# Strassen weight sums by accumulating DMAs in place of GpSimd additions in a two-layer decoder trunk

## The chip, the cores and the metric

The kernel runs on one core of a Trainium2 chip. The metric is the device time of one execution in microseconds (us); less is better. The engines are named as the profile names them: PE (TensorE, matrix products; PEld are its weight loads), DVE (VectorE), ACT (ScalarE), POOL (GpSimd) and SP (SyncE, which here only issues transfers). Each engine works through its own queue in order. Transfers between device memory and on-chip memory run on 16 shared DMA engines; an engine issues a transfer and goes on, and whoever needs the data waits on a semaphore.

## The reference

A decoder trunk of two layers on 512 tokens of width 1024, all float32. Each layer is a token mixer, a cross-attention into 256 memory tokens, and a squared-ReLU MLP with 4096 hidden channels; each is added to the residual stream after an RMSNorm.

```python
for layer in range(DEPTH):                      # DEPTH = 2
    h = h + mixer(rmsnorm(h, ...), ...)         # RG-LRU + FoX attention, or dilated + sliding-window attention
    h = h + memory_cross_attention(rmsnorm(h, ...), mem, ...)
    h = h + squared_relu_mlp(rmsnorm(h, mlp_norm[layer]), mlp_w_up[layer], mlp_w_down[layer])
return rmsnorm(h, final_norm)

def squared_relu_mlp(h, w_up, w_down):
    return jnp.square(jax.nn.relu(h @ w_up)) @ w_down
```

The change touches `h @ w_up` alone.

## The kernel before

Activations are held transposed: channels on the 128 partitions, the 512 tokens along the free axis. Every float32 product is made of three faster ones: each operand is split into a high and a low part (`hi_lo`: ACT copies it to the rounded type, L156; DVE subtracts, L157), and `mm3` issues high x high (L177), high x low (L178) and low x high (L179).

The MLP of a layer runs in four quarters of the hidden channels (`for qd in range(4)`). A quarter is four units of up-projection and then eight down-projections. A unit (class `Unit`) is a block product by a Strassen-Winograd scheme with seven products, `p1` to `p7`; its weight operands are A11, A12 and A22 (parts 0, 1 and 3 of the stored weight block) as they are loaded, and four sums formed on the chip, S1 to S4, into which part 2 goes as well. Each product is twelve matmuls of 128x128 by 128x256; each down-projection is 24 matmuls of 128x128 by 128x512. Over the kernel there are 2 layers x 4 quarters x 4 units = 32 units.

`Unit.load`, called first in `p1`, brings the weights in. It uses four tiles, each of 128 partitions:

- `d1` (printed as `wr`; 1024 columns): part 0 (A11) in the lower half, S1 in the upper. Two buffers, shared with the weight tiles of all other projections.
- `d2` and `d3` (printed as `d`; 1024 columns): A12 and S2, A22 and S4. They share four buffers (tag `v`), so that two units' pairs fit.
- `e` (printed as `ptl`; 512 columns): S3. Four buffers.

Four loads of 256 KB are issued by SP (L965). Four GpSimd additions follow (L968): S1 = part 2 + part 3, S3 = part 2 + part 0 (on top of part 2 in `e`), S2 = S1 + part 0, S4 = S2 + part 1. `Unit.weight` converts a tile when a product first asks for one of its operands: ACT to `wh`, DVE to `wl` (three buffers each). Both halves of a tile are converted by one instruction each, so a conversion of `d2` waits for A12 and S2. `d2` is asked for by `p2`, `d3` by `p4`.

The Tile scheduler sets the order of instructions on each engine from the written order and priorities; loads of weights have a raised priority (`tc.high_priority(200)`), so they stand on SP's queue as early as their buffers allow. The product steps of neighbouring units are woven into one another. In steady state, `d2` of one unit, `d2` of the next and `d2` of the third use one and the same of the four `v` buffers in turn, so that each load of `d2` waits for the conversion of the `d2` before.

Of the kernel before, what the change touches and what calls it, by code (L numbers as in the profile page):

```python
# [13 lines left out]
ALU = mybir.AluOpType  # L14
# [22 lines left out]
def build(ctx, tc, a):  # L37
    nc = tc.nc
    V, A, G, T, SY = nc.vector, nc.scalar, nc.gpsimd, nc.tensor, nc.sync
# [14 lines left out]
    def t2k(tag, dt=F32, shape=None):  # L54
        cnt[0] += 1
        return wk.tile(shape or [128, 512], dt, tag=tag, name=f"{tag}_{cnt[0]}", bufs=BUFS[tag])
# [893 lines left out]
    class Unit:  # L950
# [5 lines left out]
        def load(self):  # L956
            with tc.high_priority(200):
                cnt[0] += 1
                i = cnt[0]
                d1 = wp.tile([128, 1024], F32, tag="wr", name=f"wr_{i}", bufs=2)  # L960
                d2, d3 = (wk.tile([128, 1024], F32, tag="v", name=f"d{x}_{i}", bufs=BUFS["v"]) for x in (2, 3))
                e = t2k("ptl")
                lo, hi = slice(0, 512), slice(512, 1024)
                for part, dst in ((2, e), (3, d3[:, lo]), (0, d1[:, lo]), (1, d2[:, lo])):
                    SY.dma_start(out=dst, in_=self.src[part])  # L965
                for out, x, y in ((d1[:, hi], e, d3[:, lo]), (e, e, d1[:, lo]), (d2[:, hi], d1[:, hi], d1[:, lo]),
                                  (d3[:, hi], d2[:, hi], d2[:, lo])):
                    G.tensor_tensor(out=out, in0=x, in1=y, op=ALU.add)  # L968
            self.raw = {"d1": (d1, ("A11", "S1")), "d2": (d2, ("A12", "S2")), "d3": (d3, ("A22", "S4")), "e": (e, ("S3",))}

        def weight(self, name):
# [436 lines left out]
```

## Time and profile before

| | |
|---|---|
| device time, median of 3 runs | 1479.89 us (1478.21 to 1481.08) |
| the profiled execution | 1479.2 us, its span 1477.2 us |
| PE busy | 1425.7 us, 97% of the span |
| PE weight loads | 1234.2 us, 84% |
| DVE busy | 1073.5 us, 73% |
| ACT busy | 747.2 us, 51% |
| POOL busy | 361.9 us, 24% |
| transfers | 143.03 MB, mean 97 GB/s |

The two microseconds between the span and the execution's time lie around the span. The profile gives for each engine its busy time; the chain of waits that ended last runs over PE for 75% of the span and over DVE for 16%. The 128 GpSimd additions are among POOL's 361.9 us; POOL also does the sums of squares of the norms (L270), the last step of their roots (L298) and the division of the softmax (L348). A row of the timeline gives the start and the length of an instruction; for a transfer the length is that of its issue, and the landing is given apart.

### The profile page before, as it was taken

How to read it: one execution, taken by the hardware profiler on the slowest of the kernel's cores; microseconds unless marked ns; L12 is line 12 of the kernel's file. 1: busy time of each engine (PE TensorE's matmuls, PEld its weight loads, DVE VectorE, ACT ScalarE, POOL GpSimd, SP SyncE). 2: the span in 40 equal slices, each digit the busy share in tenths (PEclk: the TensorE clock that was granted, in tenths of full speed). 3: DMA queues.
4: the chain of work that ended last, by engine and by line, in shares of the span. 5: the costliest groups of instructions: out<-in, count | busy, mean ns of one | idle time of the engine just before them, and what ended most of it. 6: DMA issues, size and time to landing. Idle time of an engine off the chain costs nothing.

```text
span 1477.2 us, 21427 instructions
## 1 busy us (share of the span) xinstructions
PE 1425.7 (97%) x8064; PEld 1234.2 (84%) x8064; DVE 1073.5 (73%) x1733; ACT 747.2 (51%) x1321; POOL 361.9 (24%) x300
## 2 busy tenths in 40 slices
PE   7999999999899999999999999999998999999996
PEld 5777887888798989889887888788878889898985
DVE  7788876656885867678678989855497667586773
ACT  4777754545452534435457867644354435252452
POOL 3003221002613315051213313200054041422303
PEclk9999999999999999999999999999998999999998
DMA  5222214423132333422332231333222424242221
GB/s 191 83 86 86 73 65 150 136 93 129 50 115 87 117 92 87 134 58 71 110 108 69 79 94 64 100 131 126 100 93 76 125 65 128 72 122 93 72 86 57
DMA packets 55558, 143.03 MB, mean 97 GB/s; under 512 B 6816, under 2 KB 12320, under 8 KB 55456
## 3 DMA queue, kind: packets, MB, share of 16 engines
q1 hardware_dynamic: 54368, 140.63, 30.1%
q8 instruction: 63, 1.03, 0.3%
q10 hardware_dynamic: 1088, 1.05, 0.2%
q14 instruction: 39, 0.32, 0.1%
HBM read 136.15 MB, written 2.10 MB: 94 GB/s over the span
## 4 chain that ended last, share of the span: by engine, by line
PE 75%; DVE 16%; ACT 5%; issue 3%; POOL 0%; DMA 0%; DVEq 0%; ACTq 0%; POOLq 0%
PE mm L177 18%; PE mm L178 18%; PE mm L179 18%; DVE wl L157 4%; PE s L177 3%; PE s L178 2%; PE s L179 2%; PE t L354 2%; PE pv L177 1%; PE pv L178 1%; PE pv L179 1%; ACT wh L156 1%; DVE hT L474 1%; PE mm L233 1%; PE mm L234 1%
## 5 line engine op out<-in xcount | busy, mean ns | idle before, releaser
L156 ACT ACTIVATE wh<-wr 128x1024 fp32r<-128x1024 f32 x214 | 226.1, 1058 | 296.1 <-PE mm L178 224.3
L157 DVE TENSOR_TENSOR wl<-wr,wh 128x1024 fp32r<-128x1024 f32 x214 | 289.0, 1354 | 73.8 <-ACT wh L156 72.1
L177 PE MATMUL mm<-acth,wh 128*128 128x512 f32 (+1 forms) x768 | 299.1, 392 | 0.9 <-DVE hT L474 0.8
L178 PE MATMUL mm<-actl,wh 128*128 128x512 f32 (+1 forms) x768 | 297.9, 388 | 0.1
L179 PE MATMUL mm<-acth,wl 128*128 128x512 f32 (+1 forms) x768 | 297.6, 388 | 0.0
L177 PE MATMUL mm<-hgh,wh 128*128 128x512 f32 (+1 forms) x504 | 188.3, 374 | 7.6 <-ACT hgh L156 6.7
L178 PE MATMUL mm<-hgl,wh 128*128 128x512 f32 (+1 forms) x504 | 185.5, 368 | 4.7 <-DVE hgl L160 3.7
L179 PE MATMUL mm<-hgh,wl 128*128 128x512 f32 (+1 forms) x504 | 184.8, 367 | 0.3
L177 PEld LDWEIGHTS mm<-acth,wh 128*128 128x128 f32 x768 | 144.0, 188 | 30.5 <-ACT acth L156 2.0
L179 PEld LDWEIGHTS mm<-acth,wl 128*128 128x128 f32 x768 | 144.3, 188 | 29.2
L178 PEld LDWEIGHTS mm<-actl,wh 128*128 128x128 f32 x768 | 144.5, 188 | 27.7 <-DVE actl L157 0.7
L270 POOL TENSOR_TENSOR ssq<-ssq,sq 128x512 f32<-128x512 f32 (+1 forms) x48 | 67.2, 1401 | 409.2 <-ACT sq L258 408.8
L348 POOL TENSOR_SCALAR p<-p,den 128x256 f32<-128x256 f32 (+1 forms) x96 | 66.6, 699 | 254.5 <-DVE den L347 190.1
L1053 DVE TENSOR_TENSOR kv<-mm,Rt 128x512 f32<-128x512 f32 x56 | 38.7, 690 | 109.7 <-PE mm L179 109.7
L177 PEld LDWEIGHTS mm<-hgh,wh 128*128 128x128 f32 x504 | 96.5, 191 | 21.9 <-ACT hgh L156 7.1
L968 POOL TENSOR_TENSOR wr<-ptl,d 128x512 f32<-128x512 f32 x32 | 43.9, 1372 | 283.5 <-DVE wl L157 246.3
L178 PEld LDWEIGHTS mm<-hgl,wh 128*128 128x128 f32 x504 | 96.5, 192 | 18.5 <-DVE hgl L160 4.4
L179 PEld LDWEIGHTS mm<-hgh,wl 128*128 128x128 f32 x504 | 96.4, 191 | 14.6 <-DVE wl L157 0.7
L157 DVE TENSOR_TENSOR wl<-d,wh 128x1024 fp32r<-128x1024 f32 x64 | 87.0, 1359 | 22.1 <-ACT wh L156 21.8
L156 ACT ACTIVATE wh<-d 128x1024 fp32r<-128x1024 f32 x64 | 67.4, 1053 | 58.0 <-PE mm L178 42.2
L177 PE MATMUL s<-hgh,wh 128*128 128x256 f32 (+1 forms) x272 | 80.8, 297 | 3.8 <-DVE kv L1008 2.2
L179 PE MATMUL s<-hgh,wl 128*128 128x256 f32 (+1 forms) x272 | 79.7, 293 | 0.0
(322 smaller groups left out, 3297.2 us busy)
## 6 DMA issues: line engine op xcount, KB each, us to landing
wr<-in_mlp_down SPq DMA_DIRECT2D x64, 512.0 KB, 3.3
d<-in_mlp_up SPq DMA_DIRECT2D x64, 256.0 KB, 2.6
wr<-in_cd_w_in SPq DMA_DIRECT2D x18, 512.0 KB, 3.4
wr<-in_xa_q SPq DMA_DIRECT2D x16, 512.0 KB, 3.3
wr<-in_xa_k SPq DMA_DIRECT2D x16, 512.0 KB, 3.3
wr<-in_xa_v SPq DMA_DIRECT2D x16, 512.0 KB, 3.3
wr<-in_xa_w_o SPq DMA_DIRECT2D x16, 512.0 KB, 3.4
ptl<-in_mlp_up SPq DMA_DIRECT2D x32, 256.0 KB, 3.0
```

The costliest lines, as they stand in the source:

```text
L156: A.activation(out=hi, in_=src, func=AF.Copy)
L157: V.tensor_tensor(out=lo, in0=src, in1=hi.bitcast(F32), op=ALU.subtract)
L177: T.matmul(ps, lhsT=wh, rhs=xh, start=start, stop=False, **kw)
L178: T.matmul(ps, lhsT=wh, rhs=xl, start=False, stop=False, **kw)
L179: T.matmul(ps, lhsT=wl, rhs=xh, start=False, stop=stop, **kw)
L233: T.matmul(st["ps"][b], lhsT=xh, rhs=h[:, k2, :], start=k == 0, stop=False)
L234: T.matmul(st["ps"][b], lhsT=xh, rhs=lo[:, k2, :], start=False, stop=False)
L270: eng.tensor_tensor(out=self.ssq, in0=self.ssq, in1=q, op=ALU.add)
L348: G.tensor_scalar(out=p, in0=p, scalar1=dens[:, i:i + 1], scalar2=1.0, op0=ALU.mult, op1=ALU.mult)
L354: T.transpose(ps[:, c:c + 128], src, ident)
L968: G.tensor_tensor(out=out, in0=x, in1=y, op=ALU.add)
L1053: V.tensor_tensor(out=t, in0=ps, in1=Rt, op=ALU.mult)
```

## The change

The four additions go. Part 2 is loaded not only into `e` but also into the upper halves of `d1`, `d2` and `d3`, and transfers that add to what lies at their destination (`accum_op=ALU.add`), issued by GpSimd, bring the other parts on top: one for S1 (part 3), one for S3 (part 0), two for S2 (parts 3 and 0), three for S4 (parts 3, 0 and 1). Per unit there are then seven plain loads and seven accumulating transfers of 256 KB each instead of four loads and four additions; over the kernel 224 and 224 instead of 128 and 128.

```diff
--- before.py
+++ after.py
@@ -961,11 +961,10 @@
                 d2, d3 = (wk.tile([128, 1024], F32, tag="v", name=f"d{x}_{i}", bufs=BUFS["v"]) for x in (2, 3))
                 e = t2k("ptl")
                 lo, hi = slice(0, 512), slice(512, 1024)
-                for part, dst in ((2, e), (3, d3[:, lo]), (0, d1[:, lo]), (1, d2[:, lo])):
+                for part, dst in ((2, e), (3, d3[:, lo]), (0, d1[:, lo]), (1, d2[:, lo]), (2, d1[:, hi]), (2, d2[:, hi]), (2, d3[:, hi])):
                     SY.dma_start(out=dst, in_=self.src[part])
-                for out, x, y in ((d1[:, hi], e, d3[:, lo]), (e, e, d1[:, lo]), (d2[:, hi], d1[:, hi], d1[:, lo]),
-                                  (d3[:, hi], d2[:, hi], d2[:, lo])):
-                    G.tensor_tensor(out=out, in0=x, in1=y, op=ALU.add)
+                for part, dst in ((3, d1[:, hi]), (0, e), (3, d2[:, hi]), (3, d3[:, hi]), (0, d2[:, hi]), (0, d3[:, hi]), (1, d3[:, hi])):
+                    G.dma_start(out=dst, in_=self.src[part], accum_op=ALU.add)
             self.raw = {"d1": (d1, ("A11", "S1")), "d2": (d2, ("A12", "S2")), "d3": (d3, ("A22", "S4")), "e": (e, ("S3",))}
 
         def weight(self, name):
```

Several accumulating transfers to the same half-tile go one after another: each waits until the one before has landed. Lines behind L965 stand one lower in the changed kernel.

On POOL, in the second quarter of the first layer, this is the place of its third and fourth unit (790 and 807 in the names; 855 and 866 are `e` tiles, 854 the `d` tiles of the next quarter). Before:

```order
L968 TENSOR_TENSOR wr_790_4805<-ptl_791_4808,d3_790_4807 128x512
L968 TENSOR_TENSOR ptl_791_4808<-ptl_791_4808,wr_790_4805 128x512
L968 TENSOR_TENSOR d2_790_4806<-wr_790_4805 128x512
L968 TENSOR_TENSOR d3_790_4807<-d2_790_4806 128x512
L968 TENSOR_TENSOR wr_807_4940<-ptl_808_4943,d3_807_4942 128x512
L968 TENSOR_TENSOR ptl_808_4943<-ptl_808_4943,wr_807_4940 128x512
L968 TENSOR_TENSOR d2_807_4941<-wr_807_4940 128x512
L968 TENSOR_TENSOR d3_807_4942<-d2_807_4941 128x512
```

The same place on POOL now ("x2" and "x3" are so many like instructions in a row, each waiting for the one before):

```order
L967 DMA wr_790_4841<-in_mlp_up 128x512
L967 DMA d3_790_4843<-in_mlp_up 128x512 x3
L967 DMA wr_807_4982<-in_mlp_up 128x512
L967 DMA ptl_855_5455<-in_mlp_up 128x512
L967 DMA d2_790_4842<-in_mlp_up 128x512 x2
L967 DMA d3_807_4984<-in_mlp_up 128x512
L967 DMA ptl_866_5539<-in_mlp_up 128x512
L967 DMA d3_807_4984<-in_mlp_up 128x512 x2
L967 DMA d2_807_4983<-in_mlp_up 128x512
L967 DMA d3_854_5454<-in_mlp_up 128x512
L967 DMA d2_807_4983<-in_mlp_up 128x512
```

Where one addition filled a half of `d2`, two transfers in sequence do; those of `d2` stand behind the three of an earlier `d3`, and they no longer need the sum in `wr`.

On SP, the loads of the same place. Before:

```order
L965 DMA wr_790_4805<-in_mlp_up 128x512
L965 DMA d3_790_4807<-in_mlp_up 128x512
L965 DMA wr_807_4940<-in_mlp_up 128x512
L965 DMA ptl_855_5407<-in_mlp_up 128x512
L965 DMA d2_790_4806<-in_mlp_up 128x512
L965 DMA d3_807_4942<-in_mlp_up 128x512
L172 DMA wr_825_5076<-in_mlp_down 128x1024
L965 DMA ptl_866_5485<-in_mlp_up 128x512
L965 DMA d2_807_4941<-in_mlp_up 128x512
L965 DMA d3_854_5406<-in_mlp_up 128x512
```

SP now:

```order
L965 DMA wr_790_4841<-in_mlp_up 128x512 x2
L965 DMA d3_790_4843<-in_mlp_up 128x512 x2
L965 DMA wr_807_4982<-in_mlp_up 128x512 x2
L965 DMA ptl_855_5455<-in_mlp_up 128x512
L965 DMA d2_790_4842<-in_mlp_up 128x512 x2
L965 DMA d3_807_4984<-in_mlp_up 128x512 x2
L172 DMA wr_825_5124<-in_mlp_down 128x1024
L965 DMA ptl_866_5539<-in_mlp_up 128x512
L965 DMA d2_807_4983<-in_mlp_up 128x512 x2
L965 DMA d3_854_5454<-in_mlp_up 128x512 x2
```

The order on SP is the same, with two loads for each of `wr`, `d2` and `d3` where one stood. On PE, ACT and DVE the order of the products and conversions around this place is that of before but for swaps of neighbours.

## Rows read from the trace of the kernel before

**Rows 1.** Busy times by window, the second quarter of the first layer's MLP.

```profile
core 0: us, PE busy (x) PEld busy (x) DVE busy (x) ACT busy (x) POOL busy (x), PEclk, DMA share, GB/s
478.00:562.00 84.00, 83.72 (x528) 75.87 (x527) 59.45 (x68) 33.38 (x48) 25.04 (x16) 1.00 0.34 101
```

**Rows 2.** PE's waits (total, times, longest): 340 to 430 us; 430 to 700; 1110 to 1160.

```profile
PE mm L177 <- ACT hgh L156: 3.4, 1, 3.4
PE pv L177 <- DVE kv L1014: 2.6, 1, 2.6
...
PE s L177 <- DVE kv L1027: 0.4, 2, 0.3
...
PE pv L177 <- DVE kv L1014: 2.2, 1, 2.2
```

**Rows 3.** Timeline (start us, length us) of DVE around 395 us, first quarter; line totals of the additions.

```profile
392.77 0.68 DVE L157 TENSOR_TENSOR kv<-ssq,kv 128x512 fp32r<-128x512 f32 x1
393.60 2.08 DVE L157 TENSOR_TENSOR wl<-d,wh 128x1024 fp32r<-128x1024 f32 x1 [0.16 <-ACT wh L156]
395.61 1.78 DVE L157 TENSOR_TENSOR qkl<-E,qkh 128x512 fp32r<-128x512 f32 x1
...
398.74 1.75 DVE L157 TENSOR_TENSOR wh<-ptl,wh 128x512 fp32r<-128x512 f32 x1
...
L968 POOL TENSOR_TENSOR wr<-ptl,d 128x512 f32<-128x512 f32 x32 | 43.9, 1372 | 283.5 <-DVE wl L157 246.3
```

**Rows 4.** Timeline of SP, loads of `d` in quarters one (415) and two.

```profile
477.51 0.33 SPq L965 DMA_DIRECT2D d<-in_mlp_up  x1
488.39 3.11 SPq L965 DMA_DIRECT2D d<-in_mlp_up  x2
500.63 3.14 SPq L965 DMA_DIRECT2D d<-in_mlp_up  x2
...
415.13 3.12 SPq L965 DMA_DIRECT2D d<-in_mlp_up  x2
```

**Rows 5.** Transfers, issue to landing: L965's min/median/max, then medians by tile, with KB.

```profile
DMA to landing us min/median/max: 2.4/2.6/5.8
...
d<-in_mlp_up SPq DMA_DIRECT2D x64, 256.0 KB, 2.6
wr<-in_mlp_down SPq DMA_DIRECT2D x64, 512.0 KB, 3.3
kv<-in_memT SPq DMA_DIRECT2D x12, 256.0 KB, 4.1
```

**Rows 6.** Timeline of ACT and DVE: conversions of `d` in the second quarter.

```profile
486.00 1.06 ACT L156 ACTIVATE wh<-d 128x1024 fp32r<-128x1024 f32 x1 [2.30 <-PE mm L178]
498.01 1.05 ACT L156 ACTIVATE wh<-d 128x1024 fp32r<-128x1024 f32 x1
...
517.09 1.05 ACT L156 ACTIVATE wh<-d 128x1024 fp32r<-128x1024 f32 x1
...
487.10 1.23 DVE L157 TENSOR_TENSOR wl<-d,wh 128x1024 fp32r<-128x1024 f32 x1 [1.83 <-ACT wh L156]
```

**Rows 7.** Timeline of PE: first low-part matmul of `p2`, quarters two and one.

```profile
501.05 0.28 PE L179 MATMUL pv<-hgh,wl 128*128 128x256 f32 x1
511.13 0.28 PE L179 MATMUL pv<-hgh,wl 128*128 128x256 f32 x1
...
426.61 0.28 PE L179 MATMUL pv<-hgh,wl 128*128 128x256 f32 x1
```

**Rows 8.** Busy times by window around PE's longest wait; columns as in rows 1.

```profile
384.00:386.00 2.00, 0.00 (x0) 0.00 (x0) 2.00 (x4) 1.83 (x4) 0.00 (x0) 1.00 0.00 0
...
388.00:390.00 2.00, 1.53 (x7) 1.53 (x8) 2.00 (x3) 1.21 (x3) 0.00 (x0) 0.50 0.20 77
390.00:392.00 2.00, 2.00 (x11) 2.00 (x11) 1.98 (x4) 0.82 (x3) 1.53 (x1) 0.50 0.40 80
392.00:394.00 2.00, 2.00 (x15) 2.00 (x14) 1.84 (x4) 2.00 (x4) 0.99 (x1) 0.70 0.14 51
```

## The prediction

> **What bounds the kernel now.** The change lives in the eight MLP quarters, so I read one of them first. Over the 84 us of the second quarter PE is busy 83.72 us at full clock; DVE is busy 59.45, ACT 33.38, POOL 25.04, and the DMA engines have a share of 0.34 [rows 1]. So PE bounds a quarter, and relieving DVE or POOL shortens it only where PE waits for them. The list of PE's waits is the second view: from 430 to 700 us, three quarters long, the largest entry is 0.4 us. Only the first quarter of each layer has a wait that the additions could cause: `p2`'s bank `pv` waits for DVE's `kv` for 2.6 us in layer 0 and 2.2 us in layer 1. The 3.4 us for `hgh` is the norm, before any product [rows 2]. The most that the change can gain is therefore about 5 us. What it can lose is set by how far ahead of PE the weights are, and the third view is the timeline of the loads, conversions and matmuls of `d2`.
>
> **What it removes.** 128 GpSimd additions of about 1.37 us, some 176 us of POOL's time. In the first quarter DVE's conversions beside them take 2.08, 1.78 and 1.75 us. Free of them, the 128x512 form took 0.68 and the 128x1024 form takes 1.23 [rows 3, 6]. The excess of those three is 0.85 + 1.10 + 1.07 = 3.0 us, more than the wait of 2.6. I take both waits as gone, 2.6 + 2.2 = 4.8 us. The products behind them are PE's own work, and nothing else is late there. With no effect on those waits the term is 0.
>
> **What it adds on SP.** 96 more plain loads at 0.33 us of issue each [rows 4], spread over 8 x 84 us. SP waits for buffers between loads, so this costs nothing but a shift of 0.33 us for the second load of a half-tile; that shift is in the sums below. If that cover went, it would be 32 us at the very most.
>
> **What it adds on the path: serial accumulating transfers.** Half of `d2` was filled by one addition that could start as soon as its buffer came free. It now needs a load of part 2 and then two accumulating transfers, the second issued after the first has landed. Call the time from issue to landing of one such transfer L. No row shows one. The nearest rows are these: a plain load of 256 KB lands after 2.6 us; one of 512 KB after 3.3; one of 256 KB from `in_memT`, a different shape of the same size, after 4.1 [rows 5]. An accumulating transfer has to read its destination as well and is put in by GpSimd. So the low end is 2.6, and the high end two 512 KB transfers one after another, 6.6. I take 4.1, the slowest 256 KB row: same bytes, more work than the plain one. This choice is the weakest step of the whole sum.
>
> Conversion of `d2` takes 2.3 us, from ACT's start at 486.00 to DVE's end at 488.33 [rows 6], and that frees the buffer for the `d2` of the next unit. In the second quarter:
>
> - Unit 2: loads from 488.39, landed at 488.39 + 0.33 + 2.6 = 491.3, sums complete at 491.3 + 2L [rows 4, 5]. PE wants the low half at 501.05 [rows 7], so the conversion must start by 498.7 (it started at 498.01, [rows 6]). Delay 2L - 7.4, at L = 4.1 it is 0.8 us.
> - Unit 3, same buffer: the conversion ends at 493.6 + 2L, the loads land 2.9 later, and two more transfers follow: 496.6 + 4L. PE wants it at 511.13 [rows 7], conversion by 508.8. Total delay 4L - 12.2 = 4.2 us, of which 3.4 come as a second wait. If unit 2 was in time, its buffer comes free at 500.63 as before [rows 4] and the delay is 2L - 5.2, zero up to L = 2.6.
> - The first quarter has only one such step: loads from 415.13 [rows 4], sums at 418.1 + 2L, wanted at 426.61 - 2.3 = 424.3 [rows 7]. Delay 2L - 6.2 = 2.0 us.
>
> The loads have no slack of their own to hide this. They are issued the moment the buffer comes free, and a unit's twelve-matmul products go on at PE's pace. Six quarters have the two-step chain (quarters two to four of both layers, whose loads I take to repeat the pattern of rows 4): 6 x 4.2 = 25 us, plus 2 x 2.0 = 4 us.
>
> `d3` takes three transfers in a row, but is wanted later: the third unit's comes with the `d2` load at 491.2 and its conversion starts at 517.09 [rows 6]. It is not late for any L up to 6.6. On POOL, however, it is ahead of others. The `d3` of unit 2, loaded at 477.51 [rows 4], issues its third transfer at 480.4 + 2L, and the `d2` transfers of unit 2 stand behind it. At L = 4.1 that is 488.6, before 491.3, so free; at 6.6 it is 493.6, 2.3 us late, 14 us in six quarters. In the first quarter the norm's root (L298) and its sums of squares (L270) stand among the transfers on POOL, and the root is behind the last transfer to the `d2` of unit 2 there. I cost that at nothing, since the loads of that unit are the ones that find their buffers empty; without that cover it is one transfer's time, L, once a layer.
>
> **Clock.** Each PE wait of some length has a second price. After the 3.4 us wait PE ran at a granted clock of 0.50 for 4 us (388 to 392) and 0.70 for 2 us, that is 1.2 GHz and a mixture [rows 8]. It lost 4 x 0.5 + 2 x 0.3 = 2.6 us. The second wait of the chain is as long, 3.4 us, so 6 x 2.6 = 16 us. The bounds are 0, if shorter waits leave the clock alone (the 2.6 and 2.2 us waits are in the trace beside it), and 16.
>
> **The sum at L = 4.1.** 25 + 4 + 16 - 5 = +40 us on the profiled execution's 1479.2, whose own time is 0.7 below the median: 1479.9 + 40 = 1520. At L = 2.6: -5, 1475. At L = 3.5: six delays of 1.8 and two of 0.8, too short for the clock, 12 - 5 = +7, 1487. At L = 6.6: 6 x 14.2 + 2 x 7.0 = 99, + 14 + 16 - 5 = +124, 1604.
>
> The Trainium skill speaks against so large a number. Its page "Collectives: The Full Stack", section "The bandwidth ceiling: the fold count and why AG ≠ RS ≠ AR", says that an add in the transfer engines needs two source reads and so runs at half the rate of a copy. By that and the fixed cost on the page "DMA: Bandwidth & Descriptors", section "Anatomy of one DMA — SWDGE (gpsimd) path" (about 2.0 us plus bytes over 436 GB/s), I estimate L = 2.0 + 2 x 0.6 = 3.2 and a sum of 6 x 1.2 + 2 x 0.2 - 5 = +3 us. No row here shows an accumulating transfer, so I stay with 4.1.
>
> **Rivals.**
> A. *The accumulating transfer lands like a plain one, L = 2.6 to 2.7.* Then nothing of the chain is late, and the relief of DVE is all that is left: 1479.9 - 5 = 1475, faster. For it: same bytes, and 2.6 is the median of all loads of this tile. Against it: the transfer reads its destination too, and its issue is GpSimd's work. It decides at L = 2.7, where the delays begin to eat the 5 us; from 2.7 to 3.0 the result is within 0.2%. The section on the SWDGE path just named, without the second read, gives this very case: 2.0 + 0.6 = 2.6 us, an estimate.
> B. *The DMA engines fill up.* A share of 0.34 over 84 us is 28.6 us of engine time for 32 pieces of 256 KB (16 up, 16 down) [rows 1], 0.9 us each. After the change a quarter has 44 plain pieces and 28 accumulating ones. Counted once: 72 x 0.9 = 64 us, fits in 84. Counted twice: 100 pieces, 89 us, 5 us too much a quarter, 40 in all, close to the forecast's own sum. Counted 2.5 times: 114 pieces, 102 us, 18 us too much, 8 x 18 = 143, about 1620. Three times: 240 us. For it: transfers nearly double in bytes and the destination is read. Against it: the share would have to be nearly three times what it is.
> C. That the change does not do what it says is ruled out: the order on POOL holds 224 accumulating transfers and none of the 128 additions.
>
> **How the numbers follow.** The forecast (a serial chain with L above 3.0 and up to 6.6) gets 0.68, of which L = 4.1 is the likeliest; rival A 0.19 (0.10 faster, 0.09 within 0.2%, which is 3 us and about what a measurement of this kernel can tell from no change); rival B, with engines that are the bound, 0.13. Predicted 1520. The range leaves out A's faster part and half of B and of the longest L, some 0.2: 1477 to 1620. Faster 0.10, same 0.09, slower 0.81.
>
> **What would show it.** The landing time of the transfers at the changed line (4.1 forecast, under 2.8 for A). In the second quarter: PE's waits at `pv` for `wh` or `wl` of `d2`, 0.8 us and then 3.4 us with a clock of 0.5 behind it; in the first quarter one of 2 us; the old waits for `kv` gone; DVE's conversions of 128x1024 all near 1.23 us. For B: a DMA share near 1 and plain loads landing late. The forecast is wrong if L is not what I took, if the third and fourth quarter's chain differs from the second's, or if the transfers get in each other's way long before the engines are full.

## The result, and the profile after

The changed kernel takes 1621.51 us (median of 4 runs, 1614.72 to 1623.53) against 1480.49 us; the ratio is 1.094, with a 95% interval of 1.090 to 1.098. The forecast was 1520 us with a range of 1477 to 1620: slower, as forecast, but by 141 us where 40 were worked out, and just past the end of the range.

The profiled execution has a span of 1621.7 us. The first section of its page (busy us, share of the span, instructions):

```profile
PE 1463.9 (90%) x8064; PEld 1266.3 (78%) x8064; DVE 1002.2 (62%) x1733; ACT 744.5 (46%) x1321; POOL 353.3 (22%) x396
```

PE's 8064 matmuls take 1463.9 us where they took 1425.7. The span is 144.5 us longer: 38 of it are the same matmuls at a lower clock, and 106 are PE standing idle. What it waits for (engine and the bank it writes, line, producer: us in total, times, longest), over the whole span:

```profile
PE pv L177 <- ACT wh L156: 96.2, 14, 10.1
PE mm L177 <- ACT hgh L156: 10.5, 2, 5.3
PE s L177 <- DVE kv L1007: 8.2, 2, 4.5
...
PE pv L179 <- DVE wl L157: 5.4, 14, 0.5
```

Fourteen waits of `pv` for `wh`: in `p2`, for the conversion of `d2`, two in each of six quarters (15.7 us together in the second) and one in each first quarter (5.0 and 6.0), 96.2 us and 5.4 for `wl`. None of them is in [rows 2]. The old waits of `pv` for DVE's `kv` (2.6 and 2.2 us, [rows 2]) are gone; a wait of `s` for `kv` (L1007) of some 4 us in each first quarter has come (the section on why the prediction was wrong follows it up). Of the 106 us of idling, 101.6 are the waits for `d2`.

The second quarter, which the prediction was worked out for, by the same window as [rows 1]. Columns: PE, PEld, DVE, ACT and POOL busy us (instructions), granted clock, DMA share, GB/s:

```profile
478.00:562.00 84.00, 67.60 (x433) 62.68 (x432) 39.14 (x53) 27.40 (x43) 20.99 (x24) 0.88 0.76 175
```

PE does 433 matmuls in the window where it did 528, the clock is 0.88 where it was 1.00, and the DMA share is 0.76 where it was 0.34. The quarter stands some 15 us later now, by the waits before it (the loads of unit 2's `d2` are at 503.26 where they were at 488.39), so this window still holds the end of the first quarter. Moved by 15 us, to 493 to 577, it shows the same clock and 432 matmuls, and a DMA share of 0.83 at 191 GB/s.

The transfers (tile, source, issuing queue, count, KB, median us from issue to landing), and min/median/max of the accumulating ones alone. They answer to [rows 5]:

```profile
d<-in_mlp_up POOLq DMA_DIRECT2D x160, 256.0 KB, 5.7
d<-in_mlp_up SPq DMA_DIRECT2D x128, 256.0 KB, 4.1
...
DMA to landing us min/median/max: 3.8/5.7/11.1
```

L is 5.7 us and not 4.1, and the plain load before it takes 4.1 where it took 2.6.

Now the chain in the second quarter, in the timeline of SP, POOL, ACT and PE (start us, length us; in brackets the idle time before and who ended it). They answer to [rows 4, 6, 7]:

```profile
492.43 0.80 SPq L965 DMA_DIRECT2D d<-in_mlp_up  x2
...
503.26 5.15 SPq L965 DMA_DIRECT2D d<-in_mlp_up  x4
...
498.45 0.86 POOL L967 DMA_DIRECT2D d<-in_mlp_up  x1 [5.60 <-DVE wl L157]
504.22 0.86 POOL L967 DMA_DIRECT2D d<-in_mlp_up  x1 [4.91 <-DMA d<-in_mlp_up]
510.14 0.86 POOL L967 DMA_DIRECT2D d<-in_mlp_up  x1 [5.06 <-DMA d<-in_mlp_up]
510.73 1.17 POOL L967 DMA_DIRECT2D wr<-in_mlp_up  x1
511.26 1.52 POOL L967 DMA_DIRECT2D ptl<-in_mlp_up  x1
511.80 1.88 POOL L967 DMA_DIRECT2D d<-in_mlp_up  x1
520.20 1.75 POOL L967 DMA_DIRECT2D d<-in_mlp_up  x2 [6.52 <-DMA d<-in_mlp_up]
...
524.39 1.06 ACT L156 ACTIVATE wh<-d 128x1024 fp32r<-128x1024 f32 x1 [12.94 <-DMA d<-in_mlp_up]
...
525.50 0.58 PE L177 MATMUL pv<-hgh,wh 128*128 128x256 f32 x1 [10.10 <-ACT wh L156]
```

The plain loads of unit 2's `d2` are issued at 503.26 (the row's other two loads are unit 3's `d3`). The order in the section on the change says whose the POOL rows are: 498.45, 504.22 and 510.14 are the three transfers to `d3` of unit 2, the second and third issued when the one before has landed; 511.80 is the first to `d2`, 520.20 the second. The conversion starts at 524.39, 21.1 us after the loads. In the kernel before it had to start 498.7 - 488.39 = 10.3 us after them to be in time [rows 4, 7]. So it is 10.8 us late, and PE waits 10.1. The prediction said 0.8 for this step. The 21.1 us are three pieces:

- 8.5 us from the loads to the first transfer's issue, where 2.9 were counted. GpSimd's queue stood at `d3` until 510.14.
- 8.4 us from the first to the second transfer, where L = 4.1 was counted. It was issued within 1.7 us of the three before it, as soon as the queue moved.
- 4.2 us for the second transfer, as counted.

The clock behind this wait, by windows (columns as above); it answers to [rows 8]:

```profile
524.00:526.00 2.00, 0.50 (x2) 0.51 (x2) 0.52 (x1) 1.61 (x3) 0.00 (x0) 0.50 1.04 171
526.00:528.00 2.00, 1.54 (x8) 1.25 (x7) 2.00 (x3) 2.00 (x3) 0.86 (x1) 0.50 0.57 88
528.00:530.00 2.00, 2.00 (x11) 2.00 (x11) 2.00 (x4) 0.40 (x2) 0.00 (x0) 0.50 0.94 192
530.00:532.00 2.00, 2.00 (x11) 2.00 (x11) 0.24 (x1) 0.36 (x1) 0.38 (x1) 0.50 1.05 333
532.00:534.00 2.00, 2.00 (x17) 2.00 (x16) 0.69 (x1) 0.91 (x3) 1.62 (x3) 0.88 1.07 396
```

PE runs at half its clock (1.2 GHz) until about 532, as it did after the 3.4 us wait of before.

### The profile page after: what moved, and what is told of

The parts are those of the page before. It is cut to its first block, busy times and chain, and to the rows that moved or that the text cites. A ratio compares the mean times of both kernels' runs of the same rounds, so it can differ in the third digit from the quotient of the medians.

```text
span 1621.7 us, 21819 instructions
## 1 busy us (share of the span) xinstructions
PE 1463.9 (90%) x8064; PEld 1266.3 (78%) x8064; DVE 1002.2 (62%) x1733; ACT 744.5 (46%) x1321; POOL 353.3 (22%) x396
## 3 DMA queue, kind: packets, MB, share of 16 engines
q0 software_dynamic: 32256, 58.73, 22.9%
## 4 chain that ended last, share of the span: by engine, by line
PE 60%; DVE 11%; DMA 10%; issue 10%; ACT 5%; POOL 3%; SPq 0%; POOLq 0%; DVEq 0%; ACTq 0%
PE mm L177 15%; PE mm L178 15%; PE mm L179 15%; DMA d<-in_mlp_up 8%; DVE wl L157 3%; ACT wh L156 2%; DMA wr<-in_mlp_up 2%; POOL d L967 2%; PE s L177 2%; PE s L178 2%; PE s L179 1%; PE t L354 1%; PE pv L179 1%; PE pv L177 1%; PE pv L178 1%
## 5 line engine op out<-in xcount | busy, mean ns | idle before, releaser
L157 DVE TENSOR_TENSOR wl<-wr,wh 128x1024 fp32r<-128x1024 f32 x214 | 264.1, 1236 | 88.0 <-ACT wh L156 85.7
L967 POOL DMA_DIRECT2D d<-in_mlp_up x160 | 144.1, 964 | 625.9 <-DMA d<-in_mlp_up 486.6
L177 PE MATMUL mm<-hgh,wh 128*128 128x512 f32 (+1 forms) x504 | 189.0, 375 | 11.3 <-ACT hgh L156 10.5
L157 DVE TENSOR_TENSOR wl<-d,wh 128x1024 fp32r<-128x1024 f32 x64 | 77.8, 1221 | 150.6 <-ACT wh L156 150.6
L178 PEld LDWEIGHTS mm<-actl,wh 128*128 128x128 f32 x768 | 144.5, 188 | 27.8 <-DVE actl L157 0.7
L177 PE MATMUL pv<-hgh,wh 128*128 128x256 f32 x128 | 46.2, 361 | 96.6 <-ACT wh L156 96.2
L177 PEld LDWEIGHTS pv<-hgh,wh 128*128 128x128 f32 x128 | 31.8, 248 | 99.6 <-ACT wh L156 99.1
L270 POOL TENSOR_TENSOR ssq<-ssq,sq 128x512 f32<-128x512 f32 (+1 forms) x48 | 71.5, 1490 | 161.1 <-ACT sq L258 160.4
```

The lines of the kernel that those rows point to most:

```text
L157: V.tensor_tensor(out=lo, in0=src, in1=hi.bitcast(F32), op=ALU.subtract)
L177: T.matmul(ps, lhsT=wh, rhs=xh, start=start, stop=False, **kw)
L178: T.matmul(ps, lhsT=wh, rhs=xl, start=False, stop=False, **kw)
L270: eng.tensor_tensor(out=self.ssq, in0=self.ssq, in1=q, op=ALU.add)
L967: G.dma_start(out=dst, in_=self.src[part], accum_op=ALU.add)
```

## Experiments

Two theories stood after the result. The first is the forecast's: serial transfers on the way from a free buffer of `d2` to its conversion. The second is the rival that the DMA engines are full. It had gained weight: its price of 1620 us is what was measured. That price counted an accumulating transfer as 2.5 plain ones; what it takes is on the page, queue by queue (packets, MB, share of 16 engines over the span):

```profile
q1 hardware_dynamic: 68192, 165.80, 31.3%
q0 software_dynamic: 32256, 58.73, 22.9%
```

22.9% of 1621.7 us for 224 accumulating transfers is 1.66 us of all engines each, twice the 0.83 us of an average plain 256 KB in the kernel before (30.1% of 1477.2 us for 140.63 MB). Counted twice, the prediction's own sum for this rival was 40 us, and the loss is 141; but the engines' share was high enough to ask.

All times are medians; ratios are to runs of the kernel before beside them, with 95% intervals.

### S2 by GpSimd, the rest by transfers (e1), and S4 by GpSimd, the rest by transfers (e2)

Edits against the changed kernel, its lists of transfers written out one by one, e1:

```diff
-SY.dma_start(out=d2[:, hi], in_=self.src[2])
-for part, dst in ((3, d2[:, hi]), (0, d2[:, hi])):
-    G.dma_start(out=dst, in_=self.src[part], accum_op=ALU.add)
+G.tensor_tensor(out=d2[:, hi], in0=d1[:, hi], in1=d1[:, lo], op=ALU.add)
```

and e2:

```diff
-SY.dma_start(out=d3[:, hi], in_=self.src[2])
-for part, dst in ((3, d3[:, hi]), (0, d3[:, hi]), (1, d3[:, hi])):
-    G.dma_start(out=dst, in_=self.src[part], accum_op=ALU.add)
+G.tensor_tensor(out=d3[:, hi], in0=d2[:, hi], in1=d2[:, lo], op=ALU.add)
```

> S2 goes back to GpSimd's addition (S1 + A11); S1, S3 and S4 stay with accumulating transfers. Theory 1 (the chain load, two serial transfers, conversion, buffer free decides): the d2 chain has no transfer of 5.7 us left in it, so PE's waits at pv for wh of d2 (96 us in the changed kernel) are nearly gone; 1480 to 1500 us. Theory 2 (the DMA engines are full, an accumulating transfer takes 2.5 plain ones): 8 of 28 accumulating transfers and 4 of 28 loads a quarter are gone, 8 x 1.66 + 4 x 0.66 = 16 of some 79 us of engine time, so at most 141 x 16 / 45 = 50 us of the loss come back (45 us being what the quarter's engine time grew by); about 1570.

> S4 goes back to GpSimd's addition (S2 + A12); S1, S2 and S3 stay with accumulating transfers. Theory 1: the chain over d2 with two transfers each stays as it is, only its start is freed from the three transfers of d3 that stood ahead of it on GpSimd's queue; 1530 to 1580 us, clearly slower than with S2 undone. Theory 2: 12 accumulating transfers and 4 loads a quarter are gone, 12 x 1.66 + 4 x 0.66 = 22.6 us of engine time, more than with S2 undone; about 1550 and faster than that kernel.

Measured: e1 1483.58 us, 1.001 (1.000 to 1.002); e2 1573.75 us, 1.063 (1.061 to 1.065). The windows of the second quarter, e1 first:

```profile
478.00:562.00 84.00, 82.50 (x520) 74.56 (x519) 53.61 (x68) 33.02 (x48) 20.84 (x24) 1.00 0.77 186
...
478.00:562.00 84.00, 74.67 (x464) 68.50 (x463) 46.25 (x61) 30.22 (x46) 18.06 (x19) 0.92 0.65 154
```

e1's quarter stands where it stood in the kernel before. Its DMA share is 0.77 at 186 GB/s, between the changed kernel's two windows (0.76 at 175 and 0.83 at 191), and PE is busy 82.50 of 84 us. e2 has less traffic (0.65) and loses 93 us. Both came out as the first theory expected. Engines at that share are not by themselves the cause: the serial transfers of `d2` are.

### S3 alone by a transfer (e3), and seven plain loads with GpSimd's additions (e4)

Edits against the kernel before, e3:

```diff
-G.tensor_tensor(out=e, in0=e, in1=d1[:, lo], op=ALU.add)
+G.dma_start(out=e, in_=self.src[0], accum_op=ALU.add)
```

e4 has the seven plain loads of the change and the four additions (S1 on top of the part 2 that lies in `d1`).

> Only S3 is formed by an accumulating transfer, with no more plain loads than before (part 2 is in e anyway); the other three sums are GpSimd's additions. 32 accumulating transfers with little else on the queues. Both theories: no wait of PE on them, 1475 to 1483 us. What it measures is L in quiet: 3.8 to 4.2 if the 5.7 us of the changed kernel is mostly waiting for busy engines, 5 to 6 if an accumulating transfer takes that long by itself.

> Seven plain loads per unit as in the changed kernel, but the sums by GpSimd's additions as before; no accumulating transfer. Theory 1 and 2: 1478 to 1485 us, DMA share in an MLP quarter 0.34 to 0.46, landing of the plain loads 2.6 to 3. If it is slower by more than 10 us, the added plain loads are a cause of their own.

Measured: e3 1468.70 us, 0.992 (0.990 to 0.993); e4 1472.74 us, 0.995 (0.993 to 0.997). Issue to landing in e3:

```profile
DMA to landing us min/median/max: 3.8/4.1/5.3
```

In quiet, an accumulating transfer takes 4.1 us, the value the prediction took from the row of another transfer; that the two agree is luck. The estimate of 3.2 us that the prediction worked out from the Trainium skill is too short for every one of these 32 transfers (shortest 3.8). That an add needs two source reads, as the Trainium skill says on its page "Collectives: The Full Stack", section "The bandwidth ceiling: the fold count and why AG ≠ RS ≠ AR", agrees with the doubled engine time above (1.66 us against 0.83). The plain loads of e4 cost nothing. Both kernels are faster than the one before and than was expected; e3 by 12 us, more than the 5 that the prediction held to be the most, and e4 by 8 without a single accumulating transfer.

### S2 alone by transfers (e5)

```diff
-G.tensor_tensor(out=d2[:, hi], in0=d1[:, hi], in1=d1[:, lo], op=ALU.add)
+SY.dma_start(out=d2[:, hi], in_=self.src[2])
+G.dma_start(out=d2[:, hi], in_=self.src[3], accum_op=ALU.add)
+G.dma_start(out=d2[:, hi], in_=self.src[0], accum_op=ALU.add)
```

(against the kernel before)

> Only S2 is formed by accumulating transfers (a load of part 2 and two transfers in sequence); S1, S3 and S4 are GpSimd's additions. 8 accumulating transfers a quarter in place of 28. If the serial chain over the buffer of d2 costs by itself, with the quiet L of 4.1 us, the sum of the prediction applies almost as it stands: waits of PE at pv of 0.8 and 3.4 us in six quarters and 2 us in two, 29 us, up to 16 of clock, relief of at most 5: 1500 to 1525 us. If it took the traffic of all 28 transfers to make the loss, 1475 to 1485 us.

Measured: 1551.10 us, 1.048 (1.045 to 1.051). Its waits, whole span:

```profile
PE pv L177 <- ACT wh L156: 32.7, 14, 3.9
PE pv L179 <- DVE wl L157: 8.6, 14, 0.8
```

This is slower than either theory expected. With 8 of the 28 accumulating transfers a quarter, L is 4.3 us and the waits for `d2` come to 41 us; the prediction's chain gave 29 at L = 4.1. In the second quarter the two waits are 3.1 and 2.1 us. But the loss is 70 us: PE's matmuls take 1457.6 us, 32 more than before. Both waits cost clock, not the longer one alone. The windows after them:

```profile
508.00:512.00 4.00, 2.63 (x12) 2.43 (x13) 3.45 (x4) 3.48 (x6) 0.73 (x1) 0.69 0.23 79
512.00:516.00 4.00, 4.00 (x32) 4.00 (x32) 2.04 (x4) 1.29 (x3) 0.88 (x1) 0.88 0.92 251
...
524.00:528.00 4.00, 3.66 (x17) 3.37 (x17) 3.71 (x5) 1.52 (x3) 0.00 (x0) 0.50 0.46 146
528.00:532.00 4.00, 4.00 (x28) 4.00 (x28) 0.98 (x2) 1.29 (x3) 0.88 (x1) 0.75 0.92 240
```

So the chain makes half the loss with 8 of the 28 transfers.

### Six buffers for d2 and d3 (e7), and the price of that (e8)

```diff
-"v": 4
+"v": 6
-h = wp.tile([128, 1024], F32R, tag="wh", name=f"wh_{i}", bufs=3)
+h = wp.tile([128, 1024], F32R, tag="wh", name=f"wh_{i}", bufs=2)
```

(and so for every other `wh` and `wl`), on the changed kernel (e7) and on the kernel before (e8).

> The changed kernel with six buffers for d2 and d3 in place of four; the room comes from wh and wl, which have two buffers each in place of three. Same transfers and bytes as the changed kernel. If the buffer of d2 is what ties the serial transfers to the end, PE's waits at pv for wh of d2 shrink from 96 us to under 30 and the time is 1480 to 1540 us, less what two buffers for wh and wl cost. If the DMA engines are full, the waits only move: 1600 us or more.

> The kernel before with six buffers for d2 and d3 and two each for wh and wl: the price of the exchange of buffers alone. Its own waits for d2 were nil, so it cannot gain there; two buffers for wh and wl let conversions start later. 1480 to 1520 us.

Measured: e7 1554.23 us, 1.050 (1.047 to 1.053); e8 1547.25 us, 1.044 (1.042 to 1.046). Two buffers for `wh` and `wl` cost 65 us alone, more than expected, so the pair has to be read against itself: with six buffers the change costs 7 us, not 141. Its transfers are the same, L is 5.6, the DMA share in the second quarter is 0.87, and `pv` waits in e7 are down from 96.2 us to:

```profile
PE pv L177 <- ACT wh L156: 21.3, 6, 5.0
```

So with the engines busier than in the changed kernel most of the loss is gone. The reading has a weak side: a quarter of e8 is slower, which gives each chain more time.

### One transfer fewer for d2, sent to S3 (e9) or left out (e12); two of S4's sent elsewhere (e10)

Accumulating transfers, against the changed kernel; S2 is left without part 0 in e9 and e12, S4 without two parts in e10:

```diff
 (3, d1[:, hi]), (0, e), (3, d2[:, hi]), (3, d3[:, hi]), ...
-(0, d2[:, hi]), (0, d3[:, hi]), (1, d3[:, hi])
+(0, e), (0, d3[:, hi]), (1, d3[:, hi])            # e9
+(0, d3[:, hi]), (1, d3[:, hi])                    # e12
+(0, d2[:, hi]), (0, e), (1, d1[:, hi])            # e10
```

> The changed kernel with the second accumulating transfer of S2 (part 0) sent to the tile of S3 in its place, so that S2 lacks part 0 and S3 has it twice: the same 7 loads and 7 accumulating transfers of the same size, but the chain over the buffer of d2 has one transfer of 5.7 us a unit in place of two. Serial chain: each of the two steps of a quarter is 5.7 us shorter, 12 us x 6 quarters and 5.7 x 2, and its share of the clock: 1500 to 1550 us. Full DMA engines: unchanged, 1610 to 1625.

> The changed kernel with two of S4's three accumulating transfers sent elsewhere (part 0 to the tile of S3, part 1 to that of S1, so that these sums are not the right ones): same transfers and bytes, d2 keeps its two in sequence. If what counts is d2's own chain: 1600 to 1620 us. If the three transfers of d3 that stand ahead of d2's on GpSimd's queue and hold it for two landings delay the start of the chain: some 4 us less at the first wait in each of six quarters, 1575 to 1600. Full DMA engines: unchanged.

> The second accumulating transfer of S2 is left out altogether (S2 lacks part 0): as the kernel with one transfer for d2 and two for S3 (1.080), but with S3's second transfer gone from GpSimd's queue, where it held d2's for 9 us in each of the two steps. 24 accumulating transfers a quarter. If transfers that wait ahead on GpSimd's queue are the second half of the loss: 1490 to 1530 us, the first wait of quarter two at pv down from 11 to 3 us or less (only d3's three are ahead). If it is the engines' traffic: 4 of 28 transfers less, some 7 of 79 us of engine time a quarter, 1570 to 1590 us.

Measured: e9 1595.59 us, 1.080 (1.075 to 1.085); e10 1626.32 us, 1.098 (1.095 to 1.102); e12 1548.54 us, 1.045 (1.043 to 1.047). e9 misses both of its expectations: a transfer taken off `d2` gave back 26 us, not 70 or more. In e10, `d3`'s taken away gave nothing, and that is what full engines would give ("unchanged"); neither of the other two ranges was met. POOL's timeline of e9 gives another reason, which holds for both:

```profile
511.39 0.86 POOL L967 DMA_DIRECT2D d<-in_mlp_up  x1 [4.95 <-DMA d<-in_mlp_up]
512.00 1.15 POOL L967 DMA_DIRECT2D wr<-in_mlp_up  x1
512.54 1.50 POOL L967 DMA_DIRECT2D ptl<-in_mlp_up  x1
520.99 0.86 POOL L967 DMA_DIRECT2D ptl<-in_mlp_up  x1 [6.95 <-DMA ptl<-in_mlp_up]
521.53 2.11 POOL L967 DMA_DIRECT2D d<-in_mlp_up  x2
```

The transfer sent to `e` stands in the queue ahead of `d2`'s and holds it until 520.99, though `d2`'s loads were issued at 505.52. Each serial pair holds GpSimd's queue for a landing, whichever tile it is for; in e10 the pairs on `wr` and `e` hold it in place of `d3`'s. In e12, the rows of POOL, ACT and PE:

```profile
503.65 0.90 POOL L967 DMA_DIRECT2D d<-in_mlp_up  x1
512.69 1.06 ACT L156 ACTIVATE wh<-d 128x1024 fp32r<-128x1024 f32 x1 [5.34 <-DMA d<-in_mlp_up]
513.80 0.39 PE L177 MATMUL pv<-hgh,wh 128*128 128x256 f32 x1 [2.51 <-ACT wh L156]
```

The hold is gone: `d2`'s transfer is issued at 503.65, 4.5 us after the loads (499.15), and the first wait is 2.5 us in place of 11.0, as expected; the second is 2.9. The total is 47 us lower than e9's. It lies between the two expectations, above the 1490 to 1530 of the queue and below the 1570 to 1590 of the engines' traffic. Of its longer span of 72.7 us, 43 are waits of `pv` and 29 are PE's matmuls at a lower clock (1454.6 us), which the expectation had made too small again.

The first step of the second quarter in six kernels, from the timelines (us; "late" is the sum less 10.3):

| kernel | loads to first transfer | first to second | last to conversion | late | PE's longest wait there |
|---|---|---|---|---|---|
| changed | 8.5 | 8.4 | 4.2 | 10.8 | 10.1 |
| e2, S4 undone | 7.7 | 4.5 | 4.3 | 6.2 | 5.5 |
| e5, S2 alone | 3.9 | 6.1 | 4.0 | 3.8 | 3.1 |
| e9, one to S3 | 16.0 | none | 6.0 | 11.7 | 11.0 |
| e10, S4's sent elsewhere | 11.3 | 6.0 | 4.1 | 11.0 | 10.3 |
| e12, one left out | 4.5 | none | 9.0 | 3.2 | 2.5 |

The wait follows the time from load to conversion to within 0.8 us in all six. The number of transfers on `d2` alone does not set it: when the first can be issued and the length of each do. In the changed kernel, e9 and e10 the first is late by the queue; in e2 it is the plain loads, of which the second lands 7.2 us after the issue of the first. In e12 the single transfer takes 9.0 us, issued as the last of four within 2.7 us.

### Looking for a better kernel (e6, e11)

e6 forms S1 and S3 by one transfer each; e11 is e3 with part 2 loaded into `d1` too, so that the transfer onto `e` waits for no addition.

> S1 and S3 by accumulating transfers, one each; S2 and S4 by GpSimd's additions. No serial pair of transfers. If S3 alone (0.992) was faster by fewer additions beside DVE's conversions, this is as fast or faster: 1463 to 1472 us. If the addition for S2, which now waits for a transfer of 4.1 to 5 us instead of an addition of 1.4, comes late, 1475 to 1485.

> As the kernel with S3 alone by an accumulating transfer (0.992), with one more plain load: part 2 also into the upper half of d1, from where GpSimd adds part 3 for S1, so that the transfer onto e does not wait for that addition to have read e. If that wait is worth something: 1460 to 1466 us; if not, 1466 to 1472.

Measured: e6 1470.02 us, 0.992 (0.991 to 0.994); e11 1473.50 us, 0.995 (0.994 to 0.997). e6 ties with e3, so S1's transfer brings nothing beyond S3's; e11 is a little slower than e3 and than both of its expectations. The best kernel is e3, 12 us faster than the one before.

## Why the prediction was wrong in size

- **What bounds the kernel.** Right: PE, with waits in `p2` for `d2`. That the change can gain 5 us at most was too low: e3 gained 12. By its profile 4.3 of them are PE's matmuls (1421.4 us in place of 1425.7); the rest are waits: `pv` for `kv` 1.3 us in place of 4.8, `s` for `kv` 0.7 in place of 3.8, `hgh` 5.2 in place of 6.7. Only the first of these was counted.
- **Removed additions.** The two `kv` waits went, as said, and DVE's conversions of `d` take 1.22 us where they took 1.36. The 1.37 us taken for each of the 128 additions is the row of S1's alone; by the trace before, the 128 take 205 us and not 176. No term of the sum hangs on it.
- **Loads on SP.** Right: e4 has them all and loses nothing.
- **L.** This is the first step that failed. The value of 4.1 us was right for a transfer in quiet (e3) and wrong for 28 in a quarter. It is 4.1, 4.3, 4.3, 5.0 and 5.7 us in e3, e5, e2, e1 and the changed kernel, with a DMA share in the second quarter of 0.42, 0.51, 0.65, 0.77 and 0.76, and the plain loads went from 2.6 to 4.1 in the changed kernel. The step "L = 4.1" priced a transfer by a row without the traffic that the change itself brings. With L = 5.7 and loads of 4.1 the formula for six quarters is 4 x 5.7 - 12.2 + 2 x 1.5 = 13.6 us, and 2 x 5.7 - 6.2 + 1.5 = 6.7 for two: 95 us. Measured were 11.8 to 15.7 us in the six and 5.0 and 6.0 in the two, 101.6 with `wl`. That these totals are so near is in part luck: by the formula the first step of a quarter is 5.5 us late and the second 8.1 more, while the waits are 7.6 and 6.6 on average.
- **GpSimd's queue.** This is the second. The sum took `d3`'s three transfers ahead of `d2`'s as free, because 480.4 + 2 x 4.1 came before 491.3. With 6 us from the load to the first issue (492.43 to 498.45) and L of 5.8 the queue was held past the time that `d2`'s load had been counted to land. That the queue has a part of its own is what e9, e10 and e12 show.
- **The norm's root on that queue.** The prediction put it at nothing, or without cover at one L a layer. The cover was not there (POOL, then DVE, first quarter of layer 0):

```profile
408.02 0.87 POOL L967 DMA_DIRECT2D ptl<-in_mlp_up  x1 [2.41 <-DMA ptl<-in_mlp_up]
...
411.77 0.88 POOL L967 DMA_DIRECT2D d<-in_mlp_up  x1 [1.98 <-DMA d<-in_mlp_up]
412.35 1.36 POOL L298 TENSOR_TENSOR rstd<-sm,half_neg 128x4 f32<-128x4 f32 x1
...
413.74 0.16 DVE L1073 TENSOR_TENSOR r<-rstd 128x4 f32<-128x4 f32 x1 [5.40 <-POOL rstd L298]
```

The root stands behind transfers that wait for others to land, DVE waits 5.4 us for it where it waited 1.1, and DVE's L1007 stands behind that wait. So PE's `s` waits 3.8 us there and 4.5 in layer 1, 8.2 in all: two times 4.1, the price without cover. In e1, which has next to no wait for `d2`, PE's waits for the root's result (`r`) are 9.5 us where they were 1.9.
- **Clock.** Counted with 16 us, 2.6 for one wait in each of six quarters. PE's matmuls took 38 us more in the changed kernel and 32 in e5, where the waits are 1.0 to 3.9 us: 2.7 and 2.3 us for each of fourteen waits. So the price of a wait was about right and their number wrong. The prediction left waits shorter than 3.4 us out; the trace of before had one of each kind. After the `kv` wait of 2.6 us in layer 0 (PE starts at 400.9) the clock stays at 1.00, after that of 2.2 us in layer 1 (1123.5) it is 0.50:

```profile
402.00:404.00 2.00, 2.00 (x20) 2.00 (x19) 0.42 (x1) 0.02 (x1) 0.00 (x0) 1.00 0.59 189
...
1124.00:1126.00 2.00, 2.00 (x11) 2.00 (x11) 0.55 (x1) 0.00 (x0) 0.00 (x0) 0.50 0.74 154
```

The length of a wait alone does not say whether it costs clock.
- **Rival B.** Its price came out by luck, since it counted an accumulating transfer as 2.5 plain ones and two were measured; its mechanism did not: e1 runs at a like share without the loss. Traffic acts by making each transfer on the chain longer.
- **The sum again.** Of the 144.5 us of span, 101.6 are waits for `d2` (29 forecast), 38 clock (16), 8.2 the root (0) and 3.8 a longer wait for `hgh` (0), less 4.8 for the `kv` waits (5); small waits that came and went make up the remaining 2.5.

What stays open: how the landing time of 8.4 us in a burst divides between busy engines and the transfers issued just before it, and what sets whether a wait of 2 to 3 us costs clock. No run takes the three transfers of `d3` off the queue and leaves their traffic in place, so how much of the 101.6 us is the queue's and how much the longer L's is not shown.

## What to carry to other kernels

Price a transfer on the critical path by a row with the traffic that the change will bring, not by the quietest that fits, and multiply its error by the copies in the chain: here four a quarter, so that an L longer by 1.6 us is 6.4 us a quarter before any other effect. Work that waits for its own predecessor in an in-order queue delays everything behind it, so count the queue as a chain of its own. Of the seven transfers S3's alone, without a serial partner and with slack, gave the fastest kernel; S1's, also without a partner, added nothing to it (e6). How much of those 12 us is the transfer's own is not shown, since e4 gains 8 without any.

## What the runs showed of the hardware

An accumulating transfer of 256 KB takes 4.1 us from issue to landing in quiet (e3) where a plain one takes 2.6, and 1.66 us of all 16 engines (the changed kernel) where a plain one takes 0.83. GpSimd is busy 0.86 us for an issue by itself, and its 224 issues hold it nearly as long as the 128 additions did: POOL is busy 353.3 us where it was 361.9. And after waits of PE of 3.1 and 2.1 us the granted clock was at 0.69 and 0.50 in the next 4 us (e5), while after one of 2.6 us it stayed at 1.00 (the kernel before).
